# Delta rule: turning keys, queries and values to tokens by VectorE's 32x32 squares and a DMA instead of TensorE

## The chip, the cores and the metric

One core of one Trainium2 chip runs the whole program. The metric is device time in microseconds (us), the median of three runs. A profile of one execution gives for each engine what it did when: PE is TensorE (PEld its weight loads), DVE is VectorE, ACT is ScalarE, POOL is GpSimd, SP is SyncE, which here issues nearly all DMAs from one in-order queue.

## The reference, cut to what matters

A trunk of two layers on 1024 tokens of width 1024, in float32. Layer 0 mixes tokens by a gated MLP and a gated delta rule side by side; layer 1 by differential attention; behind each stand an MLP and a gated embedding. The change touches the delta rule of layer 0 alone:

```python
qkv = silu(causal_depthwise_conv(qkv, conv_w))            # 3 x 512 channels, 1024 tokens
q, k = l2_normalize(q) * d ** -0.5, l2_normalize(k)        # 4 heads of 128 channels
beta, g = sigmoid(...), -exp(a_log) * softplus(...)        # one number per token and head
gc = cumsum(g)                                             # within a chunk
decay = where(causal, exp(gc[..., :, None] - gc[..., None, :]), 0)
a = where(strict, (k * beta) @ k.T * decay, 0)
u, w = solve(a + eye, v * beta), solve(a + eye, k * beta * exp(gc))
for each chunk:                                            # the recurrence
    v_new = u - w @ state
    o = (q * exp(gc)) @ state + (q @ k.T * decay) @ v_new
    state = state * exp(gc[-1]) + (k * exp(gc[-1] - gc)).T @ v_new
```

The kernel works in 8 chunks of 128 tokens; for each chunk and head it needs keys, queries and values both as channels by tokens and as tokens by channels, and the sums of the log gates both along partitions and spread over all of them.

## The kernel before

The program is built by Python generators, and a scheduler that models time orders the instructions of each engine; the engines then run in that fixed order. Layer 0's mixing, `even_mix`, has two streams. **The fill** is the run of projections (keys, values, gate, queries, the MLP's two halves) and then the output projection: fp32 values split in a high and a low part, three matmuls for one product. `pump(n)` emits it up to unit n. **The delta rule** is emitted between pumps with a higher priority, in these steps:

- `proj_qkv` makes one head's 128 channels of 512 tokens: eight times three matmuls into a bank of PSUM, a scaled copy `cx` (VectorE), the convolution in three fused multiply-adds into a temporary `y` (VectorE), tanh (ScalarE), and the product of the silu into `qkv[i, hf]` (i is 0 for queries, 1 for keys, 2 for values; hf is the half of the tokens). Temporaries come from a pool of 4 buffers; `pg`, `pd` and `pkk` take turns in two PSUM banks.
- `gates` makes the log gates and, by matmuls `pg`, their sums `gsum`, which are also split in two parts `gparts`.
- `ahead(c)`, one for each of the 8 chunks, two pieces long. The sums are spread by 8 matmuls `pd` whose left side is a column of `gparts` broadcast over 128 columns, and ScalarE takes the exponentials from there, 8 instructions; GpSimd cuts the triangles. The keys are turned by 4 TensorE transposes `pk`; their lengths and the scaled `kt` come from them. Then `pkk` (keys by keys) is multiplied with the decay into `am` on VectorE (line 1610), and its diagonal blocks and some tiles go to DRAM (`diag`, `spill`).
- `solve` inverts all 32x32 diagonal blocks of the eight chunks at once, on VectorE; it needs `diag` of all chunks. `inverse(c)` builds the rest of the inverse from it, beginning with a VectorE transpose (line 1675) and the matmuls `py`.
- `prep(c)` turns the chunk's values (4 transposes `pv`) and queries (4 transposes `pq`, needed only for their lengths `rq`, which scale the output at the end); `step(c)` is the recurrence.

The order between the streams is held by `Ordered`: a fill matmul may stand at most LAG = 3 slots ahead of the delta rule's matmuls. In layer 1 the attention already turns its weights by VectorE's 32x32 squares and a DMA through DRAM: line 1045 transposes squares, line 1047 writes them, line 1056 reads them back with 128-byte runs so that the squares change places.

Of the kernel before, what the change touches and what calls it, by code (L numbers as in the profile page):

```python
# [18 lines left out]
P = 128  # L19
# [95 lines left out]
class Trunk:  # L115
# [3 lines left out]
    def __init__(self, tc, ctx):  # L119
        self.tc, self.nc = tc, tc.nc  # L120
        nc = self.nc
        self.cp = ctx.enter_context(tc.tile_pool(name="const", bufs=1))
        self.wp = ctx.enter_context(tc.tile_pool(name="w", bufs=2))
        self.hp = ctx.enter_context(tc.tile_pool(name="hs", bufs=1))
        self.tp = ctx.enter_context(tc.tile_pool(name="tmp", bufs=TB))
        self.sp = ctx.enter_context(tc.tile_pool(name="small", bufs=2))

        self.rp = ctx.enter_context(tc.tile_pool(name="region", bufs=1))
        self.ps = ctx.enter_context(tc.tile_pool(name="ps", bufs=2, space=PSUM))
        self.wide = ("mm",)  # L130
# [5 lines left out]
        self.identr = self.cp.tile([P, P], F32R, name="identr")  # L136
        nc.vector.tensor_copy(self.identr, self.ident)
# [1121 lines left out]
    def even_mix(self, first, rows_of_rest, rest_of_x, w_in, ws, bs, conv, a_log, dt_bias, v_gain, o_gain, masks, w_out, gain_next, h_dram):  # L1259
# [57 lines left out]
        def gates():  # L1317
            nc.scalar.activation(nea, nea, AF.Exp)
            nc.scalar.activation(hb, ba[:, :, 0:4], AF.Tanh, scale=0.5)
            nc.vector.tensor_scalar(beta, hb, 0.5, 0.5, ALU.mult, ALU.add)  # L1320
            nc.vector.tensor_scalar(hb, beta, 0.5, None, ALU.mult)
            y, e = small["nbe"], g
            nc.vector.tensor_tensor(y, ba[:, :, 4:8], bc(dtb, NC, 1), ALU.add)
            nc.vector.scalar_tensor_tensor(e, y, -1.0, y, ALU.mult, ALU.min)
            nc.scalar.activation(e, e, AF.Exp)
            nc.scalar.activation(e, e, AF.Ln, bias=self.ones[:, 0:1])
            nc.vector.scalar_tensor_tensor(e, y, 0.0, e, ALU.max, ALU.add)
            nc.vector.scalar_tensor_tensor(g, e, -1.0, bc(nea, NC, 1), ALU.mult, ALU.mult)
# [6 lines left out]
            nc.vector.tensor_copy(flat(gsum), pg[:, 0])  # L1335
# [11 lines left out]
        qkv_lo, z_lo, uv_lo = nc.vector, nc.vector, nc.vector  # L1347


        qkv, made = {}, set()  # L1350

        def proj_qkv(i, j, hfs):

            def units(w):
                for hf in hfs:
                    if (i, hf) not in qkv:
                        qkv[i, hf] = self.slot(f"A{i + 3 * hf}", [P, G, HT], F32, "qkv")
# [7 lines left out]
                    for ml in range(2):  # L1365
                        m = i * 4 + j * 2 + ml
                        ps = pss[ml] if first else self.mm_ps()
                        for k in range(0 if first else KT):
                            self.mm3(ps, w.at(k, slice(ml * P, (ml + 1) * P)), hs[hf][k], k == 0, k == KT - 1)
                            if k < KT - 1:  # L1370
                                yield None
                        cx = self.slot(f"c{10 + m % 2}", [P, 3 + HT], F32, "cx")
                        if hf:
                            nc.vector.tensor_copy(cx[:, 0:3], tails[:, m])
                        else:
                            nc.vector.memset(cx[:, 0:3], 0.0)
# [4 lines left out]
                        nc.scalar.activation(y, cx[:, 3:], AF.Copy, scale=conv[:, 3, m : m + 1])  # L1381
                        for tap in range(3):
                            nc.vector.scalar_tensor_tensor(y, cx[:, tap : tap + HT], conv[:, tap, m : m + 1], y, ALU.mult, ALU.add)
                        th = self.tmp()
                        nc.scalar.activation(th, y, AF.Tanh, scale=0.5)
                        nc.vector.scalar_tensor_tensor(qkv[i, hf][:, m % 4], th, 1.0, y, ALU.add, ALU.mult)
                        made.add((i, hf, m % 4))
                        yield None

# [183 lines left out]

        def ahead(c):

            out = []
# [4 lines left out]
            for own, other in ((gsum, 1), (nsum, -1)):  # L1581
                e = self.slot(("c6", "d0")[c % 2] if other > 0 else f"c{2 + c % 2}", [P, G, P], F32, "dec")
                for h in range(G):
                    nc.scalar.activation(e[:, h], pd[:, h], AF.Exp, scale=-float(other), bias=own[:, c, h : h + 1])
                nc.gpsimd.affine_select(e, e, pattern=[[0, G], [-other, P]], base=0, channel_multiplier=other, compare_op=ALU.is_gt if other > 0 else ALU.is_ge, fill=0.0)
                out.append(e)
            am, du = out
# [7 lines left out]
            kt = self.slot(f"c{c % 2}", [P, G, HD], F32, "kt")  # L1595
            nc.vector.tensor_tensor(kt, pt, bc(dec[:, c], HD), ALU.mult)
            keep(c, 2, kt)

            sc = self.sp.tile([P, G], F32, tag="sc", name=self.nm("sc"), bufs=3)
# [32 lines left out]
            nc.sync.dma_start(solved, flat(x))  # L1632


        mid, ch = {}, {}

        def prep(c):
            k, v = part(1, c), part(2, c)
            kt = fetch(c, 2, self.slot(f"c{c % 2}", [P, G, HD], F32, "kt"))
            du = fetch(c, 1, self.slot(f"c{2 + c % 2}", [P, G, P], F32, "dec"))  # L1640
            pt = aux([P, G, P], "tr", "pv")
            for h in range(G):
                self.pe.transpose(pt[:, h], v[:, h], self.ident)
            vb = v
            for h in range(G):
                nc.scalar.activation(vb[:, h], pt[:, h], AF.Copy, scale=hb[:, c, h : h + 1])
            yield
            q = part(0, c)
            pt = aux([P, G, P], "tr", "pq")
# [203 lines left out]
        self.pe.start(LAG)  # L1853
        solver = solve()
        systems = [ahead(c) for c in range(NC)]
        for i, n in enumerate(share(FILLA, NC + 1)):
            if i < NC:
                run(systems[i], False)
            if i:
                run(systems[i - 1], False)  # L1860
            self.pe.slot()
            pump(done + n)
        for n in share(FILLB, 10):
# [8 lines left out]
        chunk(none, invs[0], f0, FILLC, ("pi", "i", "i", "i", ""))  # L1872
        chunk(none, none, f0, 0, ("p", "p"))
        for c in range(NC):
            run(invs[c + 1], False)
# [139 lines left out]
```

## Time and profile before

| | |
|---|---|
| median of 3 runs | 2508.72 us (2507.84 to 2512.13) |
| the profiled execution | 2508.33 us; its span 2506.6 us |
| mean granted clock of TensorE | 0.999 |
| busy, whole span | PE 2486.1, DVE 1849.6, ACT 1287.2, POOL 313.9 us |
| `ahead`, all chunks | sums of gates copied at 96.36 us, the last product `am` starts at 146.41 us |
| `solve` and the first inverse | to the first `py` at 195.8 us |
| the recurrence | 8 steps; the last matmuls `pvn` start at 385.1 us |

A line of the page's parts gives busy time, share and count; a row of the windows gives for each engine the busy time in a stretch, its count in brackets, then the granted clock, the DMA engines' share and GB/s. Matmuls overlap in the records (a 128x512 one is recorded with some 400 ns while one starts every 232), so PE's busy time hides small gaps; how fast it works is read from starts and counts, which the chain of waits gives as pieces: start, length, what, count.

### The profile page before, as it was taken

What the parts mean: (1) busy time and instruction counts of PE and PEld (TensorE: products, weight loads), DVE (VectorE), ACT (ScalarE), POOL (GpSimd) and SP (SyncE); (2) the same over time, 40 slices, a digit from 0 to 9 for tenths busy, and PEclk for the clock granted to TensorE, in tenths of its full rate; (3) what the DMA queues carried; (4) which work ended last, traced back from release to release, by engine and by line L of the source; (5) the groups of instructions that cost most, each with busy time, mean ns of one, the idle gap of its engine ahead of it and who ended that gap; (6) DMA issues with size and microseconds to landing.
All of it is one profiled execution on the core that took longest, in us unless ns stands there. A gap on an engine that the chain in (4) does not pass through costs nothing.

```text
span 2506.6 us, 39970 instructions
## 1 busy us (share of the span) xinstructions
PE 2486.1 (99%) x13758; PEld 2123.8 (85%) x13758; DVE 1849.6 (74%) x3588; ACT 1287.2 (51%) x2585; POOL 313.9 (13%) x280
## 2 busy tenths in 40 slices
PE   9999999999999999999999999999999999999999
PEld 8898898888888887888899999987788888888877
DVE  7866767697667879566568888886886677787586
ACT  6543344465455444454456766664655455445452
POOL 0211232000000000000234443431000000000000
PEclk9999999999999999999999999999999999999999
DMA  7453435447565856553347776799375558655651
GB/s 236 130 159 85 134 111 179 147 155 240 173 193 208 272 175 199 184 176 117 115 99 168 158 175 154 170 251 293 127 237 191 173 184 285 209 187 189 194 178 59
DMA packets 494530, 443.05 MB, mean 177 GB/s; under 512 B 188436, under 2 KB 361464, under 8 KB 494328
## 3 DMA queue, kind: packets, MB, share of 16 engines
q1 hardware_dynamic: 494312, 440.51, 57.7%
q8 instruction: 108, 1.77, 0.3%
q14 instruction: 94, 0.77, 0.1%
q10 hardware_dynamic: 16, 0.00, 0.0%
HBM read 312.47 MB, written 127.93 MB: 176 GB/s over the span
## 4 chain that ended last, share of the span: by engine, by line
PE 94%; DVE 3%; DMA 2%; issue 1%; SPq 0%; ACT 0%; POOL 0%; DVEq 0%; ACTq 0%; POOLq 0%
PE mm L76 82%; PE po L76 3%; PE qk L76 3%; PE aux L76 2%; PE tr L79 1%; DMA raw<-in_w_ple_gate_dram 1%; DVE w L224 0%; DMA raw<-in_w_mlp_dram 0%; PE py L76 0%; PE pz L76 0%; PE aux L79 0%; PE pvn L76 0%; PE pab L79 0%; PE pkq L76 0%; PE pst L76 0%
## 5 line engine op out<-in xcount | busy, mean ns | idle before, releaser
L76 PE MATMUL mm<-g,w 128*128 128x512 f32 x2592 | 603.7, 395 | 0.9 <-DVE g L224 0.5
L223 ACT CAST w<-raw 128x512 fp32r<-128x512 f32 x598 | 365.4, 617 | 447.2 <-PE mm L76 362.4
L76 PEld LDWEIGHTS mm<-g,w 128*128 128x128 f32 x2592 | 486.3, 188 | 116.0 <-issue 1.1
L76 PE MATMUL mm<-hi,w 128*128 128x512 f32 x1728 | 555.0, 397 | 0.3 <-ACT hi L1250 0.3
L76 PE MATMUL mm<-w,hi 128*128 128x256 f32 (+2 forms) x2528 | 502.5, 295 | 0.0
L224 DVE TENSOR_TENSOR w<-raw,w 128x512 fp32r<-128x512 f32 x510 | 349.1, 692 | 179.8 <-ACT w L223 175.7
L76 PEld LDWEIGHTS mm<-w,hi 128*128 128x128 f32 x2528 | 400.1, 188 | 13.8
L76 PEld LDWEIGHTS mm<-hi,w 128*128 128x128 f32 x1728 | 325.6, 189 | 73.7 <-ACT hi L1250 0.7
L76 PE MATMUL mm<-w,lo 128*128 128x256 f32 (+2 forms) x1264 | 369.6, 293 | 0.0
L76 PE MATMUL mm<-lo,w 128*128 128x512 f32 x864 | 342.3, 396 | 0.9 <-DVE lo L1251 0.9
L76 PE MATMUL mm<-t,w 128*128 128x512 f32 x1152 | 270.8, 395 | 1.2 <-ACT w L223 1.2
L76 PEld LDWEIGHTS mm<-t,w 128*128 128x128 f32 x1152 | 216.4, 188 | 52.5 <-ACT w L223 1.6
L76 PEld LDWEIGHTS mm<-w,lo 128*128 128x128 f32 x1264 | 238.3, 189 | 5.9
L76 PEld LDWEIGHTS mm<-lo,w 128*128 128x128 f32 x864 | 163.4, 189 | 36.8 <-DVE lo L1251 1.4
L224 DVE TENSOR_TENSOR g<-graw,g 128x512 fp32r<-128x512 f32 x216 | 147.3, 686 | 9.0 <-DMA gd<-g 7.3
L223 ACT CAST g<-graw 128x512 fp32r<-128x512 f32 x216 | 132.7, 617 | 32.7 <-issue 10.1
L260 POOL TENSOR_TENSOR r<-ms,mhalf 128x4 f32<-128x4 f32 x12 | 12.9, 1076 | 1038.9 <-DVE ms L258 1010.1
L1032 ACT ACTIVATE lg<-lg,nm 128x128 f32<-128x128 f32 (+7 forms) x128 | 99.2, 775 | 76.8 <-DVE nm L1029 75.9
L224 POOL TENSOR_TENSOR w<-raw,w 128x512 fp32r<-128x512 f32 (+1 forms) x88 | 115.0, 1327 | 142.5 <-ACT w L223 75.2
L350 ACT ACTIVATE g<-g 128x512 f32<-128x512 f32 x96 | 60.5, 631 | 118.4 <-DVE g L284 114.8
L1029 DVE CUSTOM_DVE_ANT_0 lg<-qk,al 128x512 f32<-128x512 f32 (+3 forms) x128 | 74.7, 587 | 27.4 <-PE qk L76 22.0
L76 PE MATMUL mm<-ohi,w 128*128 128x512 f32 x256 | 85.9, 401 | 0.2 <-DVE t L1209 0.2
(334 smaller groups left out, 3551.6 us busy)
## 6 DMA issues: line engine op xcount, KB each, us to landing
raw<-in_w_mlp_dram SPq DMA_DIRECT2D x352, 256.0 KB, 3.3
graw<-gd SPq DMA_DIRECT2D x224, 256.0 KB, 2.8
gd<-g SPq DMA_DIRECT2D x192, 256.0 KB, 3.3
raw<-in_w_ple_gate_dram SPq DMA_DIRECT2D x76, 256.0 KB, 3.2
acc<-h_dram SPq DMA_DIRECT2D x64, 256.0 KB, 4.4
keep<-in_w_mlp_dram SPq DMA_DIRECT2D x64, 256.0 KB, 4.2
raw<-in_w_in_e_dram SPq DMA_DIRECT2D x60, 256.0 KB, 3.6
h_dram<-acc SPq DMA_DIRECT2D x48, 256.0 KB, 2.8
```

The costliest lines, as they stand in the source:

```text
L76: self._next(self.engine.matmul(*a, **k))
L79: self._next(self.engine.transpose(*a, **k))
L223: self.nc.scalar.copy(hi, src)
L224: (lo_engine or self.nc.vector).tensor_tensor(lo, src, f32(hi), ALU.subtract)
L260: nc.gpsimd.tensor_tensor(r, ms, self.mhalf[:, 0:4], ALU.pow)
L350: nc.scalar.activation(g, src, AF.Relu)
L1029: nc.vector.tensor_tensor_reduce(out=lg[:, k0:k1], in0=ps[:, : k1 - k0], in1=al[:, u0 + k0 : u0 + k1], scale=-1.0, scalar=3.0e38 if c == 0 ...
L1032: nc.scalar.activation(lg[:, :n], lg[:, :n], AF.Exp, bias=nm[:, r, nch - 1 : nch], scale=-1.0, accum_out=me.sums[:, b, r : r + 1])
```

## The change

Keys, queries and values are no longer turned by TensorE. `proj_qkv` transposes the finished 128x512 tile in 32x32 squares on VectorE into the temporary that held tanh, and writes it to DRAM (`by_token`). `read_tokens` reads a chunk back with four DMAs of 512 runs of 128 bytes, one for each block of 32 partitions, so that tokens lie on partitions: 96 such DMAs in all. Values stay in the temporary and are no longer kept as channels. The sums of the log gates are transposed once by TensorE (`pgt`), written to DRAM, and read by one broadcast DMA for each chunk into a tile `early`, from which the exponentials are taken. `ahead` has three pieces in place of two, the reads in the first; `prep` reads values and queries in its first pieces.

```diff
-        gparts = self.cp.tile([P, 2, NC, G], F32R, name="gparts")
+        g_dram = self.dp.tile([NC * G, P], F32, name="g_dram")
 ...
-            self.split(flat(gsum), flat(gparts[:, 0]), flat(gparts[:, 1]))
+            pt = aux([NC * G, P], "aux", "pgt")
+            self.pe.transpose(pt, flat(gsum), self.ident)
+            gt = self.tmp(P)[0 : NC * G]
+            nc.vector.tensor_copy(gt, pt)
+            nc.sync.dma_start(g_dram, gt)
 ...
+        def read_tokens(i, c, out):
+            hf, n = c // 4, c % 4
+            for j in range(4):
+                z = slice(32 * j, 32 * j + 32)
+                src = by_token[i, hf].rearrange("(a c) t -> c a t", c=32)[:, :, n * P + 32 * j : n * P + 32 * j + 32]
+                nc.sync.dma_start(out[z].rearrange("c h (i r) -> c h i r", r=32), src.rearrange("c (h i) r -> c h i r", i=4))
 ...
-                        nc.vector.scalar_tensor_tensor(qkv[i, hf][:, m % 4], th, 1.0, y, ALU.add, ALU.mult)
+                        if i < 2:
+                            y, y2 = qkv[i, hf][:, m % 4], y
+                        else:
+                            y2 = y
+                        nc.vector.scalar_tensor_tensor(y, th, 1.0, y2, ALU.add, ALU.mult)
+                        nc.vector.transpose(th, y)
+                        nc.sync.dma_start(by_token[i, hf][(m % 4) * P : (m % 4 + 1) * P], th)
 ...
         def ahead(c):
-            pd = aux([P, G, P], "aux", "pd")
-            for h in range(G):
-                for i in range(2):
-                    self.pe.matmul(pd[:, h], lhsT=gparts[:, i, c, h : h + 1].to_broadcast([P, P]), rhs=self.identr, start=i == 0, stop=i == 1)
+            if c == 0:
+                early.extend(self.slot(t, [P, 4, HT], F32, "early") for t in ("A0", "A3"))
+            du, kt = (e[:, c % 4].rearrange("p (h t) -> p h t", h=G) for e in early)
+            nc.sync.dma_start(flat(du), g_dram[G * c : G * c + G].rearrange("h t -> (h t)").partition_broadcast(P))
+            read_tokens(1, c, kt)
+            yield
+            yield
 ...
-            pt = aux([P, G, P], "tr", "pk")
-            for h in range(G):
-                self.pe.transpose(pt[:, h], k[:, h], self.ident)
-            rk = inverse_length(pt, "rk", self.slot(f"c{4 + c % 2}", [P, G, HD], F32, "sq"))
-            nc.vector.tensor_tensor(kt, pt, bc(dec[:, c], HD), ALU.mult)
+            rk = inverse_length(kt, "rk", self.slot(f"c{4 + c % 2}", [P, G, HD], F32, "sq"))
+            nc.vector.tensor_tensor(kt, kt, bc(dec[:, c], HD), ALU.mult)
 ...
         def prep(c):
-            for h in range(G):
-                self.pe.transpose(pt[:, h], v[:, h], self.ident)
+            read_tokens(2, c, vb)
+            if c == 0:
+                yield
 ...
-            for h in range(G):
-                self.pe.transpose(pt[:, h], q[:, h], self.ident)
-            rq = inverse_length(pt, "rq", self.slot(("d0", "c6")[c % 2], [P, G, HD], F32, "sq"))
+            read_tokens(0, c, qt)
+            yield
+            rq = inverse_length(qt, "rq", qt)
 ...
-        for i, n in enumerate(share(FILLA, NC + 1)):
+        for i, n in enumerate(share(FILLA, NC + 3)):
```

The scheduler's order changes inside `even_mix` and hardly outside it. TensorE's order in `ahead`, about chunk 3 to 4, before the change (`mm` is fill, `pd`, `pkk` the chunk's spread sums and key products, `pv` the turning of chunk 0's values):

```order
L76 MATMUL mm_1579<-lo_539,w_1170 128x512
L76 MATMUL mm_1579<-hi_538,w_1171 128x512
L79 MATMUL pv_2348<-ident,qkv_426 128x128 x3
L76 MATMUL mm_1579<-hi_585,w_1244 128x512
L76 MATMUL mm_1579<-lo_586,w_1244 128x512
L76 MATMUL mm_1579<-hi_585,w_1245 128x512
L76 MATMUL pd_1504<-identr,gparts 128x128 x8
L76 MATMUL pkk_1546<-qkv_691 128x128 x4
```

And the same place with the change:

```order
L76 MATMUL mm_1507<-lo_636,w_1179 128x512
L76 MATMUL mm_1507<-hi_635,w_1180 128x512
L76 MATMUL pkk_1548<-qkv_703 128x128 x4
L76 MATMUL mm_1676<-hi_327,w_1099 128x512
L76 MATMUL mm_1676<-lo_328,w_1099 128x512
L76 MATMUL mm_1676<-hi_327,w_1100 128x512
```

Only fill and key products are left between two chunks. VectorE's order in `ahead` before, ahead of a chunk's product `dec<-pkk` (`l`, `sc`, `carved` belong to key lengths and gates, `t` to a convolution):

```order
L1561 TENSOR_REDUCE l_307_1621<-sq_1619 128x4
L1596 TENSOR_TENSOR kt_1626<-pk_1614,carved_242 128x512
L1379 COPY carved_242<-cx_1566 128x3
L1602 TENSOR_TENSOR carved_242<-sc_1541,carved_242 128x4
L1561 TENSOR_REDUCE l_317_1692<-sq_1690 128x4
L1596 TENSOR_TENSOR kt_1697<-pk_1685,carved_242 128x512
L1562 TENSOR_SCALAR l_307_1621<-l_307_1621 128x4
L1383 SCALAR_TENSOR_TENSOR t_1570<-cx_1566,cols,t_1570 128x512
L1562 TENSOR_SCALAR l_317_1692<-l_317_1692 128x4
L1610 SCALAR_TENSOR_TENSOR dec_1355<-pkk_1475,sc_1383,dec_1355 128x128 x4
```

With the change, a piece with one of the squares' transposes ahead of a product:

```order
L1407 SCALAR_TENSOR_TENSOR t_1361<-t_1366,t_1361 128x512
L1400 SCALAR_TENSOR_TENSOR t_1496<-cx_1492,cols,t_1496 128x512
L1408 STREAM_TRANSPOSE t_1366<-t_1361 128x512
L1400 SCALAR_TENSOR_TENSOR t_1496<-cx_1492,cols,t_1496 128x512
L1629 SCALAR_TENSOR_TENSOR dec_1389<-pkk_1469,sc_1410,dec_1389 128x128 x4
L1400 SCALAR_TENSOR_TENSOR t_1496<-cx_1492,cols,t_1496 128x512
L222 TENSOR_TENSOR w_1514<-raw_1511,w_1513 128x512
L222 TENSOR_TENSOR w_1683<-raw_1680,w_1682 128x512
L1391 COPY cx_1721<-carved_240 128x3
L1407 SCALAR_TENSOR_TENSOR t_1496<-t_1501,t_1496 128x512
L1400 SCALAR_TENSOR_TENSOR t_1626<-cx_1623,cols,t_1626 128x512
```

This transpose turns values, and the instructions of its convolution stand around the product. In all, 8 transposes stand on VectorE ahead of the copy of the gates' sums, 6 between it and the last product, and 10 behind. SyncE's order in `ahead`, before (`raw` is a weight):

```order
L1613 DMA diag<-dec_1442 32x4x32 x4
L1568 DMA spill<-dec_1442 128x512
L1568 DMA spill<-dec_1519 128x512
L101 DMA raw_2203<-in_w_in_e_dram 128x2x256
L1613 DMA diag<-dec_1513 32x4x32 x4
```

And with the change, where the second half's keys have just been written:

```order
L1409 DMA by_token_702<-t_1231 128x512
L1632 DMA diag<-dec_1311 32x4x32 x2
L1591 DMA spill<-early_1143 128x512
L1632 DMA diag<-dec_1311 32x4x32 x2
L1365 DMA early_1144<-by_token_702 32x16x32 x8
L1602 DMA early_1143<-g_dram 128x512
L1591 DMA spill<-early_1143 128x512
L1365 DMA early_1144<-by_token_702 32x16x32 x3
```

The reads of keys stand among writes that wait for VectorE's products.

More of the change, by code (lines that the diff above doesn't have):

```diff
@@ L135, in __init__ @@
         make_identity(nc, self.ident)
-        self.identr = self.cp.tile([P, P], F32R, name="identr")
-        nc.vector.tensor_copy(self.identr, self.ident)
         self.ones = self.cp.tile([P, 1], F32, name="ones")
@@ L1347, in even_mix, with home @@
         qkv_lo, z_lo, uv_lo = nc.vector, nc.vector, nc.vector
-        qkv, made = {}, set()
+        qkv, made, by_token = {}, set(), {}
+        def home(i, hf):
+            if (i, hf) not in qkv:
+                qkv[i, hf] = self.slot(f"A{i + 3 * hf}", [P, G, HT], F32, "qkv")
+        def read_tokens(i, c, out):
+            hf, n = c // 4, c % 4
+            assert all((i, hf, m) in made for m in range(G))
+            for j in range(4):
+                z = slice(32 * j, 32 * j + 32)
+                src = by_token[i, hf].rearrange("(a c) t -> c a t", c=32)[:, :, n * P + 32 * j : n * P + 32 * j + 32]
+                nc.sync.dma_start(out[z].rearrange("c h (i r) -> c h i r", r=32), src.rearrange("c (h i) r -> c h i r", i=4))
         def proj_qkv(i, j, hfs):
@@ L1355, in units @@
                 for hf in hfs:
-                    if (i, hf) not in qkv:
-                        qkv[i, hf] = self.slot(f"A{i + 3 * hf}", [P, G, HT], F32, "qkv")
+                    if (i, hf) not in by_token:
+                        by_token[i, hf] = self.dp.tile([G * P, HT], F32, name=self.nm("by_token"))
+                        if i < 2:
+                            home(i, hf)
                     first = (i, hf, j) == (1, 0, 0)
@@ L1385, in units @@
                         nc.scalar.activation(th, y, AF.Tanh, scale=0.5)
[L1386 removed]
+                        if i < 2:
+                            y, y2 = qkv[i, hf][:, m % 4], y
[4 more added lines that the diff above has]
+                        nc.sync.dma_start(by_token[i, hf][(m % 4) * P : (m % 4 + 1) * P], th)
                         made.add((i, hf, m % 4))
@@ L1855, in even_mix @@
         systems = [ahead(c) for c in range(NC)]
-        for i, n in enumerate(share(FILLA, NC + 1)):
[L1857 to L1860, printed above, removed]
+        for i, n in enumerate(share(FILLA, NC + 3)):
+            for j in range(min(i, NC - 1), max(0, i - 3) - 1, -1):
+                run(systems[j], False)
             self.pe.slot()
@@ L1871, in even_mix @@
         f0 = prep(0)
-        chunk(none, invs[0], f0, FILLC, ("pi", "i", "i", "i", ""))
+        chunk(none, invs[0], f0, FILLC, ("pi", "i", "i", "i", "p"))
         chunk(none, none, f0, 0, ("p", "p"))
```

24 lines of the change are left out of this document (9 added, 15 removed).

## The prediction, on record before the changed kernel ran

> **What bounds the kernel now.** I read the page's first and fourth parts, then the windows, then the chain of waits by pieces, and last the single engines' timelines where the delta rule is made. Busy time by engine, and what the chain that ended last is made of:
>
> ```profile
> PE 2486.1 (99%) x13758; PEld 2123.8 (85%) x13758; DVE 1849.6 (74%) x3588; ACT 1287.2 (51%) x2585; POOL 313.9 (13%) x280
> ...
> PE 94%; DVE 3%; DMA 2%; issue 1%; SPq 0%; ACT 0%; POOL 0%; DVEq 0%; ACTq 0%; POOLq 0%
> ```
>
> TensorE sets the end nearly everywhere. So a TensorE instruction taken away is worth its whole time, unless another engine is as full in that stretch. The windows show that. Their columns are the stretch, its length, and busy time of PE, PEld, DVE, ACT and POOL; then clock, DMA share and GB/s. The stretches are: up to the copy of the gates' sums, from there to the last product of `ahead`, and the recurrence.
>
> ```profile
> 36.00:96.36 60.36, 60.36 (x381) 54.21 (x380) 50.61 (x109) 31.40 (x56) 7.18 (x6) 1.00 0.43 129
> 96.36:147.50 51.14, 48.97 (x309) 43.47 (x308) 45.17 (x122) 31.55 (x92) 18.46 (x24) 0.97 0.57 178
> 190.00:390.00 200.00, 199.41 (x1754) 181.34 (x1753) 143.04 (x351) 84.10 (x192) 52.48 (x53) 1.00 0.36 106
> ```
>
> In the recurrence VectorE has 57 of 200 us free. In `ahead` it has 6.0 of 51.1, and TensorE is close to full too: two engines share the bound. The change lightens one of them and loads the other.
>
> **What goes from TensorE.** Pieces of the chain of waits (start, length, count) give the price of a group, and the groups by form give the counts:
>
> ```profile
> 111.33 0.84 PE pd L76 x8
> 118.10 0.46 PE pk L79 x4
> 146.31 49.59 PE mm L76 x385
> 237.21 0.59 PE pq L79 x4
> 261.90 0.59 PE pv L79 x4
> ```
>
> ```profile
> L76 PE MATMUL pd<-identr,gparts 128*128 128x128 f32 x64 | 8.2, 270 | 0.0
> L79 PE MATMUL pq<-ident,qkv 128*128 128x128 f32 x32 | 5.6, 287 | 0.0
> L79 PE MATMUL pv<-ident,qkv 128*128 128x128 f32 x32 | 5.3, 279 | 0.0
> L79 PE MATMUL pk<-ident,qkv 128*128 128x128 f32 x32 | 5.2, 275 | 0.0
> ```
>
> `pd`: 8 groups of 8 at 0.84 are 6.7 us. `pk`: 8 groups of 4 at 0.46 are 3.7. `pv` and `pq`: 16 groups at 0.46 to 0.59, 7.4 to 9.4; I take 0.50, since part of a 0.59 is the change from a matmul of another kind that any neighbour would pay: 8.0. Together 18.4 (17.8 to 19.8). One transpose `pgt` comes, at most 0.12. About 10.4 us of this lie in or before `ahead`, with one `pv` group (0.5); 7.5 lie in the recurrence.
>
> **What comes to VectorE.** Twenty-four transposes of 128x512. The attention does the same already, so the trace has the row; the other rows are those whose counts change in `ahead` (mean ns behind the busy time):
>
> ```profile
> L1045 DVE STREAM_TRANSPOSE lg<-lg 128x512 f32<-128x512 f32 x8 | 5.7, 707 | 0.1
> ```
>
> ```profile
> L224 DVE TENSOR_TENSOR w<-raw,w 128x512 fp32r<-128x512 f32 x101 | 70.0, 700 | 30.1 <-ACT w L223 29.4 <-PE mm L76 0.3
> L1383 DVE SCALAR_TENSOR_TENSOR t<-cx,cols,t 128x512 f32<-128x512 f32 x72 | 56.2, 781 | 4.7 <-ACT t L1381 4.0
> L1386 DVE SCALAR_TENSOR_TENSOR qkv<-t,t 128x512 f32<-128x512 f32 x24 | 17.6, 734 | 4.1 <-ACT t L1385 4.0
> L1561 DVE TENSOR_REDUCE l<-sq 128x4 f32<-128x512 f32 x16 | 10.8, 678 | 0.0
> L1596 DVE TENSOR_TENSOR kt<-pk,carved 128x512 f32<-128x512 f32 x8 | 5.5, 684 | 0.1
> ```
>
> 24 x 0.707 are 17.0 us: 8 stand ahead of the copy of the gates' sums, 6 between it and the last product, 10 behind. The Trainium skill, "VectorE: DVE Perf Modes", in its rules for kernel authors, has 128x128 transposed on TensorE wherever PSUM may take the result; that speaks against this change. Four squares cost TensorE 0.46 to 0.59 here and VectorE 0.707, which agrees, but the rows also say that TensorE is the fuller engine. By that rule alone the sum would be 17.0 less 18.4 and a loss as soon as VectorE cannot hide its part.
>
> **`ahead`, step by step.** Between the copy and the last product the order has 6 transposes and 3 fused operations more, 2 reductions, 2 products of keys and 1 weight part fewer. So VectorE needs 45.2 + 6 x 0.707 + 3 x 0.76 - 2 x 0.68 - 2 x 0.68 - 0.70 = 48.3 us, of a stretch that lasted 51.1. It cannot become much shorter, whatever TensorE saves. Three moments fix the rest: the copy, the last product, and the transpose and matmuls that open the first inverse.
>
> ```profile
> 96.36 0.19 DVE L1335 COPY carved<-pg 128x32 f32<-128x32 f32 x1
> ...
> 146.41 1.13 DVE L1610 SCALAR_TENSOR_TENSOR dec<-pkk,sc,dec 128x128 f32<-128x128 f32 x4 [0.28 <-DMA diag<-dec]
> ```
>
> ```profile
> L1675 DVE STREAM_TRANSPOSE inv<-inv x8: 299/311/315, 191.1 to 370.0; 128x128 f32<-128x128 f32 x8
> ...
> L76 PE MATMUL py<-inv,am x128: 184/191/213, 195.8 to 370.7; 32*32 32x32 f32 x128
> ```
>
> Ahead of the copy come 8 transposes, 2 reductions and 2 key products and a weight part, less two silu products that go behind it: 7.6 us; the stretch before it had 60.36 - 50.61 = 9.75 us idle. Nearly all is hidden; I let the copy be 1.0 late, between 0 and 7.6. The way of the gates' sums grows by a transpose, a write and a read: with 2.2 and 2.9 us to landing below, some 6 us, of which the order covers all but about 1.5. The last product then ends at 96.4 + 1.0 + 48.3 + 1.5 = 147.2, where it ended at 147.5: as before.
>
> TensorE does win a little: its last key products need the banks freed by the product of two chunks earlier, and between that and the end VectorE has four fused operations, a transpose, two products and small ones, 6.5 us, so it goes on at 140.7. Then come 0.9 of key products and, by the order, 400 fill matmuls (385 before, in 49.59 us), 51.5 us: `py` at 193.1 instead of 195.8. The inverse's data, ready at 191.1 + 0.3 before, are ready then as well. **Kept in `ahead`: 2.7 us of 10.4**; the bounds are the whole 10.4, and a loss where VectorE ends later, which is priced under the rivals.
>
> **The reads.** A tile's read is four DMAs of 64 KB in 128-byte runs on SP's queue. The attention's reads have such runs; beside them a 256 KB weight with long runs, a write, a read of a spilled tile, and what one issue costs on SP:
>
> ```profile
> raw<-in_w_mlp_dram SPq DMA_DIRECT2D x352, 256.0 KB, 3.3
> ...
> aT<-a_dram SPq DMA_DIRECT2D x48, 256.0 KB, 3.7
> ...
> spill<-dec SPq DMA_DIRECT2D x16, 256.0 KB, 2.2
> ...
> dec<-spill SPq DMA_DIRECT2D x8, 256.0 KB, 2.9
> ...
> aT<-a_dram SPq DMA_DIRECT2D x16, 64.0 KB, 2.9
> ```
>
> ```profile
> L1056 SPq DMA_DIRECT2D aT<-a_dram x96: 359/378/3857, 1279.8 to 1712.4; - x96
> ```
>
> Four issues at 0.38 and 2.9 to landing: a chunk's keys are there 4.4 us after SP begins, against pieces of `ahead` some 5 us long and two of them between read and use. Values of the first half have the whole of `solve`. Queries are read only for their lengths, which the output needs, not the recurrence. So the reads cost nothing while SP is on time; 129 more issues are some 50 us of SP in 350. The Trainium skill, "DMA: Bandwidth & Descriptors", wants 512 bytes in a run for full rate; 3.7 against 3.3 us for 256 KB shows little of that here.
>
> **The recurrence.** Behind `py` VectorE gets 10 transposes, 7.1 us, on 143 of 200: hidden. TensorE's 15 groups go, 7.5 us, and nothing else is near its bound. **Kept: 7.5 us** (7 to 9; less if a step waits).
>
> Sum: 2508.33 - 2.7 - 7.5 = 2498.1; the median of the runs stands 0.4 above the profiled execution, so 2498.5.
>
> **Rivals.**
> *All of it is kept*, since VectorE's fill work moves into `solve` and `ahead` shrinks with TensorE: 2508.3 - 18.4 + 0.1 = 2490. Against it stands VectorE's 45.17 of 51.14.
> *VectorE takes it back.* Its 7.1 us in the recurrence show as waits and `py` comes at 195.8 as before: 2508.3 - 7.5 + 7.1 = 2508. The same comes out if the reads of the second half's keys are slow and end `ahead` a few us late.
> *Slower: the temporaries.* A transposed tile now holds one of 4 temporaries until its write has landed, and that write stands in SP's queue behind products. SP's waits for these:
>
> ```profile
> SPq L1613 <- DVE dec L1610: 10.8, 6, 4.1
> ```
>
> On average 1.8 us of wait and 2.2 to landing, 4.0 for each of the six tiles in `ahead`. If all six hold up the next convolution in turn, VectorE stands 24 us, less the 2.8 it has over 48.3: the last product is 21 late. The inverse, ready at 191.4, is ready at 212.6, and `py` is 16.8 later than 195.8; less 7.5, the kernel ends at 2517.6. It decides from `py` later than 195.8 + 7.5 = 203.3, a last product over 12 us late. For it: VectorE is the fullest there; against it: a head needs two temporaries and four exist, and the uv tiles already wait so for their writes.
>
> **Chances.** The forecast 0.42, all kept 0.10, taken back 0.22, slower 0.26. About 0.2% (5.0 us) is what a measurement of this kernel can tell from no change: the first two are faster, 0.52; the third within, 0.22; the last slower, 0.26. The range 2489 to 2515 leaves out the far side of "all kept" and about half of the slower case.
>
> **What would show it.** Right: VectorE near 48 us busy between the copy and the last product, that product at 145 to 150 us, small waits of TensorE before `pkk`, `py` about 193, and the recurrence shorter by 7 to 8. Wrong: a last product before 142 (all kept) or after 155, VectorE or ScalarE idle in `ahead` behind a write of squares, or steps of the recurrence that wait for a read.

## The result, and the profile after

The changed kernel took 2525.07 us, the median of 4 runs (2523.13 to 2529.31); the kernel before took 2509.84 beside it. The ratio is 1.0063, with a 95% interval of 1.0050 to 1.0075: slower by some 15 us, where 10 us faster was forecast. The profiled execution is the longest of the four, 2529.31 us with a span of 2527.6.

The page of the kernel after, busy time and the chain that ended last:

```profile
PE 2480.6 (98%) x13599; PEld 2113.7 (84%) x13599; DVE 1867.0 (74%) x3611; ACT 1289.1 (51%) x2584; POOL 316.5 (13%) x280
...
PE 87%; DVE 4%; DMA 4%; SPq 2%; issue 1%; ACT 1%; POOL 0%; DVEq 0%; ACTq 0%; POOLq 0%
```

TensorE's instructions went as planned, yet its busy time fell by 5.5 us only (2486.1 to 2480.6), not by 18.3; and the span less the busy time, which is TensorE's idle time, rose from 20.5 to 47.0. These two are the whole difference of the spans: 26.5 - 5.5 = 21.0 us. The windows say where. Columns: stretch, its length, busy time of PE, PEld, DVE, ACT, POOL, granted clock, DMA share, GB/s. First the kernel before:

```profile
96.00:150.00 54.00, 51.83 (x331) 46.28 (x330) 46.16 (x122) 33.67 (x95) 18.46 (x24) 0.97 0.57 178
150.00:200.00 50.00, 50.00 (x386) 47.36 (x385) 32.02 (x86) 14.77 (x30) 0.20 (x1) 1.00 0.47 142
200.00:470.00 270.00, 268.41 (x2079) 238.11 (x2078) 193.69 (x441) 116.23 (x247) 66.39 (x62) 1.00 0.42 128
```

The same stretches of the kernel after, and the stretch from its copy of the gates' sums to its last product:

```profile
96.00:150.00 54.00, 37.05 (x171) 30.99 (x170) 43.23 (x112) 28.39 (x73) 16.88 (x21) 0.83 0.72 205
150.00:200.00 50.00, 46.69 (x375) 46.49 (x375) 30.55 (x92) 19.96 (x53) 4.56 (x7) 0.95 0.72 201
200.00:470.00 270.00, 264.41 (x2041) 233.39 (x2041) 198.94 (x448) 110.00 (x234) 66.20 (x62) 0.99 0.52 148
```

```profile
102.32:160.37 58.05, 41.10 (x224) 36.25 (x223) 45.47 (x122) 31.10 (x84) 18.14 (x23) 0.82 0.75 212
```

`ahead` now lasts 58.05 us instead of 51.14. VectorE is busy in 45.5 of them, TensorE in 41.1 at a clock of 0.82: neither is full. And a lower clock stretches what TensorE does: one chunk's key products (`pkk`) take 1.05 us from 115.38 on, at a granted clock of 1.00; another's, behind a wait, take 1.91 from 110.05 on, at 0.50. Busy time times (1 - clock) is 6.3 us in the first of the three windows, 2.3 in the second, 2.6 in the third, against 1.6 in the three of before. By this estimate 9.7 of the 12.8 us that TensorE's busy time did not fall are slower matmuls; the other 3.1 are not placed.

The moments of the forecast, by line and by tile (minimum, median and longest duration in ns, then first and last start), after:

```profile
L1333 DVE COPY carved<-pg x1: 183/183/183, 102.3 to 102.3; 128x32 f32<-128x32 f32 x1
...
L1629 DVE SCALAR_TENSOR_TENSOR dec<-pkk,sc,dec x32: 336/343/353, 115.8 to 160.0; 128x128 f32<-128x128 f32 x32
...
L76 PE MATMUL py<-inv,am x128: 191/191/212, 211.0 to 417.4; 32*32 32x32 f32 x128
```

Copy 102.3, first product 115.8, last product 160.0, `py` 211.0; before they stood at 96.4, 107.4, 147.2 and 195.8. The last transpose of the mixing (`pab<-ident,qkv`) is taken below as the end of the recurrence; it started at 459.0 before and at 472.7 after. Behind it the code is the same, and the profiles of the kernels of this study differ there by up to 7 us; so the moments up to it, and the medians, carry the argument. Of the 21.0 us between the two profiles 13.7 lie up to it; the medians are 15.2 apart.

TensorE's waits after, from 60 to 165 us and from 165 to 470 (us in total, times, longest):

```profile
PE pkk L76 <- DVE dec L1629: 11.8, 2, 10.0
PE pws L79 <- DMA t<-in_gmlp_ws_dram: 5.1, 1, 5.1
...
PE mm L76 <- ACT w L221: 3.3, 1, 3.3
PE mm L76 <- DVE alo L1557: 2.9, 1, 2.9
```

Before, the first stretch had 2.2 us of this kind. The first two rows, 11.8 and 5.1 us, make up all of TensorE's 16.95 us of idle time between 96 and 150. The 5.1 us are for the spatial gate's weights: SyncE issues their read at 105.04, and in the kernel before at 73.33. In e1, the run below with the sums alone, it is issued at 100.32 and nobody waits, and in the run with the keys alone nobody waits either. So this wait comes from the parts together, and no run isolates it. Some pieces of the chain of waits behind them (start, length):

```profile
101.80 0.60 DVE early L1615
102.40 0.10 DVE carved L1333
...
104.73 0.27 DVE t L1337
...
105.55 4.29 DMA g_dram<-t
109.86 3.44 DMA early<-g_dram
...
125.88 5.04 DMA by_token<-t
130.98 0.30 SPq L1365
...
138.38 3.14 DMA early<-by_token
...
174.29 2.38 DMA qkv<-by_token
176.84 1.28 ACT qkv L1669 x4
178.11 0.52 ACT w L221
```

Where the chain was mostly TensorE's matmuls, it is now a string of DMAs: the sums' write and read, the write of the last key tile of the second half, SyncE's issues of its reads, and values that ScalarE has to scale before it comes to a weight's cast. SyncE's queue shows the holds (start, length of the row, instructions):

```profile
76.90 9.19 SPq L1365 DMA_DIRECT2D early<-by_token  x16
...
130.98 4.02 SPq L1365 DMA_DIRECT2D early<-by_token  x8
...
164.92 11.98 SPq L1365 DMA_DIRECT2D qkv<-by_token  x16
```

### The profile page after: what moved, and what is told of

Read it like the earlier page. It is cut to its first block, busy times and chain, and to the rows that moved or that the text cites. A ratio compares the mean times of both kernels' runs of the same rounds, so it can differ in the third digit from the quotient of the medians.

```text
span 2527.6 us, 39880 instructions
## 1 busy us (share of the span) xinstructions
PE 2480.6 (98%) x13599; PEld 2113.7 (84%) x13599; DVE 1867.0 (74%) x3611; ACT 1289.1 (51%) x2584; POOL 316.5 (13%) x280
## 4 chain that ended last, share of the span: by engine, by line
PE 87%; DVE 4%; DMA 4%; SPq 2%; issue 1%; ACT 1%; POOL 0%; DVEq 0%; ACTq 0%; POOLq 0%
PE mm L76 77%; PE po L76 3%; PE qk L76 2%; PE aux L76 2%; SPq L1365 1%; PE tr L79 1%; DVE w L222 1%; DMA raw<-in_w_ple_gate_dram 1%; DMA aT<-a_dram 0%; DMA a_dram<-lg 0%; PE pgm L76 0%; DVE t L1400 0%; DVE acc L282 0%; DMA by_token<-t 0%; SPq L1632 0%
```

## The experiments

Three theories were set against one another. **Q**: SyncE's queue, that is, the round trips and the order in which writes, reads and spills stand behind each other. **V**: VectorE's 17.0 us of squares. **G**: the longer way of the gates' sums. The table gives each run, the median of the kernel before beside it, and the ratio with its interval; "off PE" is the TensorE time that the kernel saves by the prices of the prediction.

```
kernel               off PE   median    before    ratio [95%]
changed kernel         18.3   2525.07   2509.84   1.0063 [1.0050, 1.0075]
e4_dead                 0     2509.50   2509.88   1.0001 [0.9993, 1.0009]
e5_nodve               18.3   2525.96   2508.92   1.0063 [1.0050, 1.0077]
e1_sums                 6.7   2515.49   2509.88   1.0023 [1.0014, 1.0032]
e2_keys                 3.7   2521.45   2509.88   1.0044 [1.0032, 1.0056]
e3_qv                   8.0   2512.19   2509.88   1.0008 [1.0000, 1.0017]
e7_ceiling             18.4   2496.95   2508.92   0.9949 [0.9935, 0.9963]
e6_onedma              18.3   2535.61   2508.92   1.0103 [1.0089, 1.0117]
e9_longruns            18.3   2528.54   2509.62   1.0071 [1.0058, 1.0084]
e10_poolq              18.3   2547.01   2509.62   1.0144 [1.0128, 1.0160]
e8_qv_onedma            8.0   2510.73   2508.92   1.0006 [0.9998, 1.0015]
e11_sums_pre            6.7   2504.90   2509.62   0.9981 [0.9972, 0.9990]
e12_q                   4.0   2507.97   2509.62   0.9990 [0.9981, 0.9998]
e13_keys_half           1.9   2512.05   2509.26   1.0014 [1.0005, 1.0022]
e14_no_trip             3.7   2516.38   2509.26   1.0029 [1.0019, 1.0040]
e17_keys_4dec           3.7   2509.56   2510.07   0.9997 [0.9988, 1.0006]
e18_before_4dec         0     2510.47   2510.07   1.0003 [0.9994, 1.0012]
e15_sums_q             10.7   2500.31   2509.26   0.9962 [0.9949, 0.9974]
e16_sums_q_khalf       12.6   2510.13   2509.26   1.0005 [0.9996, 1.0014]
```

And the moments in the profiles (us): first and last product, first `py`, last `pab`.

```
kernel           first   last    py      pab
before           107.4   147.2   195.8   459.0
changed kernel   115.8   160.0   211.0   472.7
e7_ceiling       104.6   141.4   192.5   446.0
e1_sums          110.0   152.5   202.6   461.7
e11_sums_pre     109.6   146.4   194.2   455.5
e2_keys          112.8   154.0   201.4   468.1
e17_keys_4dec    113.9   148.4   197.7   458.7
e3_qv            107.4   148.2   196.9   458.4
e12_q            108.1   147.3   195.7   455.3
e15_sums_q       109.2   145.9   193.9   447.5
```

### VectorE's squares by themselves, and the change without them

```
e4_dead, on the kernel before:
+ nc.vector.transpose(th, qkv[i, hf][:, m % 4])
e5_nodve, on the changed kernel:
- nc.vector.transpose(th, y)
- nc.sync.dma_start(by_token[i, hf][...], th)
+ nc.sync.dma_start(by_token[i, hf][...], y)
```

> The kernel before with 24 squares of VectorE added whose results nobody reads: no DMA, no change on TensorE. It prices VectorE's 17.0 us alone. Theory V: 14 of the 24 stand ahead of the last product, where VectorE had 6 us free of 51: last product 4 to 10 us later, 2514 to 2520. Theories Q and G: VectorE hides them, 2509 to 2512.

> The changed kernel with VectorE's 24 squares left out and everything else kept: the untransposed tiles are written, and read back by the same DMAs (so keys, queries and values are not turned to tokens, and the output is another). Theory Q (SyncE's queue, the issues and the round trips): the loss stays, 2520 to 2526. Theory V (VectorE's 17 us): most of it goes, 2505 to 2514.

The window of the products in e4, then in e5:

```profile
96.00:150.00 54.00, 52.22 (x339) 46.98 (x338) 48.41 (x130) 33.45 (x95) 20.43 (x24) 0.97 0.57 178
```

```profile
96.00:150.00 54.00, 39.48 (x203) 33.20 (x203) 42.36 (x115) 27.81 (x71) 15.65 (x21) 0.87 0.71 203
```

Theory V falls from both sides. With 24 squares more, VectorE is busy 48.4 of 54 us and TensorE loses nothing; without them the whole loss stays.

### The three parts alone

```
e1_sums:  before, with the new gates() and the read of du from g_dram; pk, pv, pq stay
e2_keys:  before, with by_token for i == 1 and the read of kt; pd, pv, pq stay
e3_qv:    before, with by_token for i != 1 and the new prep(); pd, pk stay
```

> The kernel before with the sums of log gates alone taken through DRAM (keys, queries and values stay on TensorE, so no 32x32 squares and no key reads; ahead keeps its three stages). pd's 6.7 us of TensorE go. Theory Q (SyncE's queue and the round trips of the squares cost the time): the sums are not the culprit; 2503 to 2507, last product by 150 us. Theory V (VectorE's 17 us of squares): the same, 2503 to 2507. Theory G (the sums' own round trip, and the spatial gate's weights that are now issued behind waiting DMAs, delay the first products): first product (L1629 in after) at 113 to 116 instead of 107.4, 2511 to 2518.

> The kernel before with the keys alone through squares and DRAM (gates' sums stay on TensorE, queries and values stay on TensorE). pk's 3.7 us of TensorE go; 8 squares of VectorE and 8 reads of four DMAs come. Theory Q: chunk 4's product waits some 10 us for its keys as in after, last product 155 to 160 us, 2514 to 2522. Theory V: 8 x 0.707 = 5.7 us on VectorE, some of it hidden: 2508 to 2513. Theory G: the loss is not here, 2506 to 2510.

> The kernel before with queries and values alone through squares and DRAM (ahead's keys and sums stay on TensorE). pv's and pq's 8.0 us of TensorE go; 16 squares and 16 reads of four DMAs come. Theory Q: the reads hold SyncE 9 to 12 us four at a time and delay weights and fetches in the recurrence; 2506 to 2511. Theory V: 16 x 0.707 = 11.3 us on VectorE, 6 of them in or before ahead: 2508 to 2514. Theory G: nothing of the loss is here; the full 8 us are kept, 2501 to 2503.

By their times e1 falls into G's range, though its first product, at 110.0, is earlier than G had it; e2 falls into Q's; e3 lies above Q's range and inside that of V, which e4 and e5 had already ruled out, so it decides nothing alone. Every part costs more than it saves: 6.7 + 5.6 = 12.3 us for the sums, 3.7 + 11.6 = 15.3 for the keys, 8.0 + 2.3 = 10.3 for queries and values. Together that would be 19.5 us slower; the whole change is 15.2, so they overlap a little. Q expected the sums to be harmless; they are not. Waits from 96 to 160 us in e1, and a piece of its chain:

```profile
PE pkk L76 <- DVE dec L1611: 7.9, 1, 7.9
...
ACT dec L1587 <- DMA spill<-early: 3.2, 1, 3.2
```

```profile
120.56 3.90 DMA spill<-early
...
124.48 0.34 SPq L1581
```

L1581 is the read of the sums of a later chunk. Its place holds the tile of four chunks earlier until that is spilled. The spill, issued at 120.56, takes 3.9 us to land; SyncE issues three diagonal blocks meanwhile and then stands from 122.5 to 124.5, with diagonal blocks and spills of other chunks queued behind the read.

### What the saving is worth when nothing replaces it

```
e7_ceiling, on the kernel before: pd, pk, pv, pq left out;
  exponentials of a constant tile, lengths and products of k, q, v as they stand
```

> The kernel before with pd, pk, pv and pq left out and nothing in their place (no sums spread, keys, queries and values not turned to tokens; the rest reads what is there). It is what the saved TensorE instructions are worth when their replacement is free. If TensorE's time is worth its whole length: 2490 to 2493 (18.4 us). If the fill work's own VectorE chains take over as soon as TensorE is shorter: 2497 to 2504.

At the lower edge of the second expectation: 12.0 us of 18.4 are kept, with nothing in the place of what went. The recurrence keeps its 7.5 and more (from `py` to the last `pab` 253.5 us against 263.2). But `py` is only 3.3 earlier, although 10.9 us of TensorE's work are gone in or before `ahead` and VectorE is busy in only 43.8 of the 54 us from 96 to 150. Between 96 and 160 us ScalarE waits 11.4 us for `spill<-dec`, which is no less than in the changed kernel, and TensorE waits behind it:

```profile
PE pkk L76 <- DVE dec L1603: 4.3, 1, 4.3
```

So in `ahead` the trace points to the two tiles `dec`, of which more below, and not to the fill work's VectorE; no run left the work out and had four of them. The forecast of 2498.5 stood 1.5 us short of what the change gives when its replacement is free.

### Issues, runs and the engine that issues

```
e6_onedma:    squares over tokens 4c+j, one DMA of 256 KB for a read instead of four
e9_longruns:  four DMAs for a read, 512-byte runs, nothing put in order
e10_poolq:    the reads of by_token and g_dram by nc.gpsimd instead of nc.sync
e8_qv_onedma: e3 with e6's reads
```

> The changed kernel with one DMA for a read instead of four: the squares are taken over every fourth token, and the tokens of a chunk lie together in DRAM, so that partition 4c+j reads at one stride. The same bytes in the same 128-byte runs, 24 issues instead of 96. Theory Q, if the issues are the cost: SyncE is held 2 to 5 us where it was held 9 to 12, last product by 152 us, 2512 to 2518. Theory Q, if the bytes and short runs are the cost: as after, 2521 to 2527. Theory G (the sums' way): 2519 to 2525, since their write, read and late weights are untouched.

> The changed kernel with reads of the same size and number, but of 512-byte runs: each of the four DMAs of a read brings one head's 128 features of a chunk as they stand in DRAM (so nothing is put together as tokens, and the output is another). Theory Q by the number of issues: SyncE is held as long as in after, 2520 to 2527. Theory Q by short runs: an issue costs 0.4 us instead of 0.5 to 2.8, chunk 4's keys come 5 us earlier, 2513 to 2520.

> The changed kernel with the reads of squares and of the sums issued by GpSimd instead of SyncE. Theory Q by order (writes of diag, spills and weights stand behind reads in SyncE's queue): 2510 to 2518, SyncE free of the holds at 131 to 138 and 165 to 177 us. If GpSimd, which also makes the triangles of every chunk, is held by its reads instead: 2522 to 2535.

> Queries and values alone through squares and DRAM (as in the run with only these), with one DMA for a read instead of four. Theory Q, issues: the four-at-a-time hold of SyncE goes, 2503 to 2508. Theory V (10 squares of VectorE in the recurrence stand on the chain of the spatial gate's fill work): 2510 to 2514, no better than with four.

None of the first three helps; each is slower than every range expected of it. In e9 an issue takes less at its longest (min, median, longest ns; in the changed kernel the values' reads had 430/487/2783), but one wait before a product is the longest of the study:

```profile
L1363 SPq DMA_DIRECT2D qkv<-by_token x32: 319/430/1675, 60.4 to 332.1; - x32
```

```profile
PE pkk L76 <- DVE dec L1627: 20.1, 3, 19.7
```

In e10 GpSimd, which makes the triangles, issues the reads; a row of 16 takes it as long as it took SyncE, and four products wait:

```profile
77.98 10.47 POOL L1365 DMA_DIRECT2D early<-by_token  x16 [3.51 <-DMA by_token<-t]
```

```profile
PE pkk L76 <- DVE dec L1629: 22.8, 4, 9.9
```

Each edit also lets the scheduler order the instructions anew, and in e6 that shows: reads of values stood between the blocks of the products, and the issue of one spill, at 149.99, took 4.6 us. Its loss of 26.7 us is therefore not the price of one DMA a read alone, and e8, which reads so without the keys, is level with e3 (by its time inside V's range again, above Q's). So fewer issues do not help the queries and values, and longer runs do not help the whole; for the keys the number of issues was not tried by itself. What moves with the three is where SyncE's or GpSimd's queue stands still, which is argued from their rows.

### Sums without the stop, and queries alone

```
e11_sums_pre, on e1: all eight chunks read behind the write, in three DMAs
+ if c == 0:
+     for e, at, n in ((0, 0, 1), (0, 1, 3), (1, 0, 4)):
+         nc.sync.dma_start(early[e][:, at : at + n]..., g_dram[...].partition_broadcast(P))
- nc.sync.dma_start(flat(du), g_dram[G * c : G * c + G]...)
e12_q, on the kernel before: by_token for i == 0 only, read by one DMA, for rq
```

> The kernel before with the sums of log gates alone taken through DRAM, as in the run with only these, but read for all eight chunks at once, in three DMAs behind their write, so that no later read stands in SyncE's queue waiting for a spill to land. Theory Q by order: the 7.9 us wait before pkk goes and most of pd's 6.7 us are kept, 2503 to 2508. Theory G (the round trip itself, 6 us from the sums' copy to the first triangle): 2508 to 2513.

> The kernel before with the queries alone through squares and DRAM, one DMA for a read; only their lengths are taken from it, which nothing in the recurrence waits for. 8 groups of pq (4.0 us of TensorE) go. Theory Q: with 8 reads instead of 16 or 24 and nobody waiting, 2505 to 2508. If a read's hold of SyncE costs by itself, whoever waits for its data: 2508 to 2512.

Both fall into Q's ranges, e12 at the edge. In e11 it is the same part, the same bytes, but no read that waits for a spill: 2515.49 becomes 2504.90, and the 7.9 us before `pkk` become 2.5:

```profile
PE pkk L76 <- DVE dec L1613: 2.5, 1, 2.5
```

The first product still comes at 109.6 instead of 107.4: theory G's way is real, and costs 2 us where e1 had lost 12.3. The queries, for which nothing waits, gain 1.7 by the medians and 3.7 by the last `pab`, of 4.0 saved.

### Keys: late, or held?

```
e13_keys_half, on e2: by_token and reads for hf == 0 only; pk for c >= 4
e14_no_trip, on e2:   read_tokens(1, c % 4, kt) instead of read_tokens(1, c, kt)
```

> The kernel before with the keys of the first four chunks alone through squares and DRAM; chunks 4 to 7 keep their pk on TensorE. If the loss of all keys through DRAM (2521.5) is the second half's round trip, made just before it is needed: 2507 to 2511. If it is the reads' hold of SyncE, half of it stays: 2514 to 2518.

> All keys through squares and DRAM, with every write and read kept, but chunks 4 to 7 read the first half's tile, which landed long before (their keys are then another chunk's, and the output is another). Round trip: the wait before chunk 4's product goes, 2506 to 2512. Hold of SyncE by issues and bytes: 2518 to 2523, as with all keys.

Neither expectation holds clean. Without the second half's round trip a third of the loss goes (2516.4); with half of the keys a quarter to a third stays (2512.1), and e13's profile shows none of it up to the last `pab` (457.8 against 459.0), so that rest is not placed. What passes both on to TensorE is the ring of two tiles `dec`: a chunk's exponentials need the tile of two chunks earlier, which is free when SyncE has issued four diagonal writes and a spill and the spill has landed. The wait for it from 96 to 160 us, before, in e2 and in the changed kernel:

```profile
ACT dec L1584 <- DMA spill<-dec: 4.0, 2, 2.4
...
ACT dec L1612 <- DMA spill<-dec: 8.8, 3, 6.0
...
ACT dec L1609 <- DMA spill<-dec: 11.8, 4, 3.8
```

The last two runs took nearly all of that wait away and left every DMA in place:

```
e17_keys_4dec, on e2:               am = early[1][:, c % 4]   (tile "A0", four chunks)
e18_before_4dec, the same on before: e  = early[0][:, c % 4]
- am = self.slot(("c6", "d0")[c % 2], [P, G, P], F32, "dec")
```

> All keys through squares and DRAM, every DMA kept, but the triangles stand in four tiles instead of two, so that a chunk's exponentials need not wait for the spill of two chunks earlier. If the ring of two tiles, stretched by SyncE's delays, is what passes them on to TensorE: 2509 to 2514, and ScalarE's wait for spill<-dec gone. If the keys' lateness itself is: 2517 to 2522, as with two tiles.

> The control: the kernel before with the triangles in four tiles instead of two. It waited 4.0 us for spill<-dec, with 2.2 us of TensorE's own: 2506 to 2510.

The window of the products in e2, and TensorE's wait:

```profile
96.00:150.00 54.00, 47.38 (x270) 40.91 (x269) 46.49 (x121) 31.78 (x91) 18.04 (x23) 0.94 0.65 185
...
PE pkk L76 <- ACT dec L1612: 4.9, 3, 3.3
```

e17, its waits from 96 to 160 us and the window of the products:

```profile
ACT dec L1612 <- DMA spill<-dec: 1.2, 2, 0.7
PE pkk L76 <- ACT dec L1612: 0.8, 1, 0.8
```

```profile
96.00:150.00 54.00, 51.83 (x325) 46.26 (x324) 49.92 (x133) 35.99 (x98) 21.02 (x25) 0.97 0.61 175
```

2521.45 becomes 2509.56, TensorE's busy time in the window is again that of the kernel before, and the control does not move. With the keys read from DRAM, all squares and all DMAs kept, two more tiles give the 12 us back. The keys are no earlier for it: SyncE issues the last chunk's reads from 133.24 on in e2 and from 135.50 on in e17, and still the last product starts at 148.4 instead of 154.0. What four tiles do not give is a gain: e17 and e18 differ by 0.9 us, within their noise, for 3.7 saved. And the whole change was not run with four tiles.

### What gains together

```
e15_sums_q:        e11 and e12 together
e16_sums_q_khalf:  the same, and keys of chunks 0 to 3 by one DMA each
```

> The two parts that gained alone put together: sums of log gates read for all chunks at once (2504.9), and queries through squares with one DMA a read (2508.0). If they add: 4.7 + 1.6 = 6.3 below the kernel before, 2502 to 2505. If SyncE or the fill work's own chains bound what TensorE can give: 2505 to 2508.

> The same, and the keys of the first four chunks through squares and DRAM as well, one DMA a read. If only the second half's round trip was at fault, 1.8 us of pk more: 2500 to 2504. If any read in the stretch of the products costs: 2505 to 2512.

e15 beats both kernels, and the better of its two expectations: 2500.31 us, 9.0 below the median of the kernel before beside it, for 10.7 saved, with VectorE at 1854.4 us and the chain at TensorE again:

```profile
PE 2474.5 (99%) x13663; PEld 2111.4 (85%) x13663; DVE 1854.4 (74%) x3595; ACT 1288.1 (52%) x2584; POOL 316.3 (13%) x280
...
PE 93%; DVE 3%; DMA 2%; issue 1%; SPq 1%; ACT 0%; POOL 0%; DVEq 0%; ACTq 0%; POOLq 0%
```

The first half's keys on top take all of it back (e16), still with two tiles `dec`; four beside the sums' eight places would need room that was not looked for.

## Why the prediction was wrong

**The step that failed** is the one on the reads: "So the reads cost nothing while SP is on time". It priced one chunk's read alone, 4.4 us. The last square of the second half's keys ended at 121.5, its write was issued at 125.88 and had landed at 130.9; chunk 4's keys were in use from 134.96, 13.5 us behind the square, and those of chunk 6, with reads issued until 138.4, landed at 141.5, 20 us behind it. And SyncE was not on time for others either. Pieces of the timelines of VectorE, ScalarE, SyncE and ScalarE again:

```profile
120.77 0.70 DVE L1408 STREAM_TRANSPOSE t<-qkv 128x512 f32<-128x512 f32 x1
...
134.96 0.63 ACT L1582 ACTIVATE sq<-early 128x512 f32<-128x512 f32 x1
...
137.85 0.49 SPq L1591 DMA_DIRECT2D spill<-dec  x1
...
141.31 1.28 ACT L1609 ACTIVATE dec<-early,carved 128x128 f32<-128x128 f32 x4 [3.44 <-DMA spill<-dec]
```

The spill at 137.85 stands behind eleven reads of keys. It frees the tile for chunk 4's triangle, whose exponentials begin at 141.31; chunk 4's product follows at 145.77, and it ends TensorE's wait of 10.0 us. The stretch from the first product to the last grew from 39.8 to 44.2 us, where the kernel with four tiles needs 34.5 with the keys by DMA and 36.6 without.

**VectorE's bound of `ahead`** was well counted and did not bind: 48.3 us forecast, 45.5 measured, in a stretch of 58.05. The forecast took the fuller engine as the limit; the limit was a ring of two tiles with a DMA in it, which no busy share shows. That is shown for the keys alone, by e17; for the whole change it is read from the trace. The wait `ACT dec` for `spill<-dec`, 4.0 us, already stood in the trace of before. And e7 shows that the first premise, a TensorE instruction taken away being worth its whole time unless another engine is as full, was too simple: 12.0 of 18.4 us are kept, and no other engine is as full.

**The copy** was put 1.0 late, within 0 to 7.6; it was 5.9 late. The squares are not the reason (96.7 in e4, 96.9 in e1); in e2 and e13 it is at 102.0 and 101.6, and in e7, without squares and reads, at 100.9. The keys' reductions and products, freed from TensorE, run ahead of it, as the sum had listed them, and the 9.75 us of idle time did not take them in.

**The sums' way**, put at 1.5, is 2.5 (copy to first product 13.5 against 11.0; 13.2 in e11). A small miss; but the wait for the spill, 7.9 us in e1, was not seen.

**`py`** was to be 2.7 earlier and is 15.2 later. **The recurrence** was to keep 7.5: from the last product to the last `pab` the changed kernel needs 312.7 us, before 311.8. The price was right, for e7 needs 304.6 and the queries alone 308.0. It is the values that give it back: with them (e3) 310.2, though 4.0 us more are saved. In the changed kernel their reads hold SyncE 12 us, ScalarE waits 15.3 us for them in seven waits, and a weight's cast behind it costs TensorE 3.3. Which of their waits costs what in the later chunks was not isolated.

**The clock** was left out of the sum: every wait was priced at its length. Of 18.3 us of instructions taken away TensorE's busy time gave back 12.8, and by the estimate above 9.7 of them are slower matmuls.

**The rivals.** The slower case had the right sign, and its mark came true, a `py` later than 203.3; its mechanism was the wrong one: in the changed kernel no engine waits for a temporary until its write of squares has landed, and e5, where VectorE makes no squares, is as slow. "Taken back" had named slow reads of the second half's keys, which is nearest to what happened, but gave them a few us; the keys alone cost 15.3. "All kept" at 2490 is more than even e7 gives. The rule of the Trainium skill, "VectorE: DVE Perf Modes", rules for kernel authors, came out right in its verdict for keys (no gain even with four tiles) and values, but e4 shows that VectorE's time is not the reason here, and the queries in e12 and e15 are the exception: nobody waits for them.

## What to carry to other kernels

When work moves from a full engine to DMA, follow each tile through its ring of buffers before adding up busy time: how many there are, which DMA frees one, and what stands ahead of that DMA in its queue. A read that waits for a buffer stops everything queued behind it, so read early into places of its own, or move only what nobody waits for. Leaving the work out altogether, and adding the new load with nobody using it, are two cheap runs that give the ceiling and the cover before anything is built.

## What the runs showed of the hardware

- With long waits of TensorE the granted clock was lower: behind the two waits of 5.1 and 10.0 us it stood at 0.50 (109.9 to 111.9 and 146.9 to 149.0), and from 96 to 150 us the changed kernel had TensorE busy for 37.05 us at 0.83, e16 for 44.72 at 0.94, e18 for 52.76 at 1.00. Idle time alone does not fix it: e13 with 49.77 and e15 with 50.30 busy also show 1.00, and the kernel before with 51.83 shows 0.97.
- A row of 16 reads of 64 KB in 128-byte runs held SyncE for 9.19 and 11.98 us, 0.57 to 0.75 us each, where 0.38 was forecast from reads issued in ones and twos; the same row took GpSimd 10.47 us.
- Twenty-four squares of 128x512, 17 us of VectorE, cost nothing measurable (1.0001, 0.9993 to 1.0009), though VectorE was busy in 48.4 of 54 us.
